# Layer 1's first head: three projections in one group, the gate after them

## The chip, the cores and the metric

The kernel runs on one core of a Trainium2 chip. The metric is the device time of one execution in microseconds (us); a comparison is the ratio of two such times. TensorE multiplies matrices, VectorE, ScalarE and GpSimd work on tiles, SyncE's queue starts the transfers. In the rows of the profile they are PE (PEld is its weight load), DVE, ACT, POOL and SP.

## The reference

Two layers of a hybrid decoder act on 512 prompt tokens and 32 sample tokens (8 sequences of 4), 544 columns in all, with a model width of 1024. Layer 0 is block-sparse attention beside a convolution branch and one output projection. Layer 1, where the change lies, is a gated linear recurrence with eight heads of 128 channels. Cut to what matters here:

```
h = rms(x, norm_1)
q, fz, i, g = split(h @ w_in_1, [1024, 1024, 1024, 1024])
f = lb + (1 - lb) * sigmoid(fz);  kk = 1 - f;  qq = silu(q);  vv = i
o, S = scan(qq, kk, log f, vv, S0)          # chunks of 64 tokens, per head
y = x + (rms(o, o_norm_1) * silu(g)) @ w_out_1
```

For each head the four projections (q at column 0, forget gate f at 1024, value v at 2048, output gate g at 3072) are 1024 by 128 matrices applied to all 544 columns.

## The kernel before

Activations lie transposed, channels on the 128 partitions and tokens along the free axis, in two halves of 272 columns. A projection is done by `unit(w, a, hf)` for one half: 24 matmuls of 128x128 by 272 columns that add up in one PSUM bank of the tag g. There are three per block of 128 input channels: high part of the weights by high part of h, high by low, low by high. Tag g has three banks, used in turn, so a unit waits until the unit three places before it has been read out of its bank.

`wtile` brings one weight matrix in: a transfer into `wr`, the rounded high part `wh` by ScalarE (L133), the rest `wl` by VectorE (L134). Each of the three has three buffers, used in turn, so a `wh` conversion waits until the last matmul that read the matrix three places before it.

The end of layer 0 sets how layer 1 starts. Half 0 of x is finished first and normalized (`normed`, L167 and L105/L106) while the output projection of half 1 runs. Half 1 is not normalized at first: h holds x times the norm's weight, split raw (L645, L646), and the scale per token, `r1b`, comes when the sum of squares has gone through one matmul with ones (L655), a square root on ScalarE (L656) and a reciprocal (L657). So in the first head of layer 1 each result of half 1 is scaled on its way out of PSUM (L745, which writes a tile named `sg`). After the first head `normed(lp, "n1", r1b, 1)` (L749) overwrites half 1 of h with the normalized values, eight blocks of each part, which the second head needs.

`proj(hd)` runs four jobs in two groups of two. In each group it goes by halves: job a half 0, job b half 0, job a half 1, job b half 1:

```
jobs = ((1024, ep_f), (0, ep_q), (2048, ep_v), (3072, ep_g))
for grp in (jobs[:2], jobs[2:]):
```

What follows a unit is its `ep_` function. `ep_f` and `ep_q` need ScalarE's sigmoid (L714, L720), `ep_v` is a plain copy (L735), `ep_g` a sigmoid and a product (L731, L732). The sigmoid is in another table of ScalarE than the square root of L656 and the exponential of L673 (a small softmax for `lb`); a table is loaded by an ACT_TABLE_LOAD.

`scan(hd)` is the recurrence. It starts with products on VectorE (L771 to L810), then come four runs of small matmuls (L818, L824, L826, L829: `kk` by `qy`, `kv` by `qx`, the sample states), then VectorE multiplies `kk` and `qq` by decays for rising block sizes (L888, L887), ScalarE keeps copies of them at two sizes (L851, L852) and scales the eight sample states (L930, after L829), and more small matmuls follow (L859 and on). GpSimd does one product `ve` (L932) per head, after `vx` (L707).

The order on each engine is fixed when the kernel is built: a scheduler follows the program's order as priority and places each instruction where its own timing model finds it ready. Engines run their lists in order. The order printed for a kernel tells what stands behind what; no time is read from it.

Of the kernel before, what the change touches and what calls it, by code (L numbers as in the profile page):

```python
# [66 lines left out]
def hybrid_step(ctx, tc, xt_in, cache_kt, cache_v, conv_in, hgrn_in, page_table, par_in, k_norm_0,  # L67
# [15 lines left out]
    def mk(pool, tag, shape, bufs, dt=F32):  # L83
        return pool.tile(shape, dt, name=nm(tag), tag=tag, bufs=bufs)

    def bank(tag, cols=512, dt=F32):
        return pp.tile([128, cols], dt, name=nm(tag), tag=tag, bufs={"g": 3, "s": 2, "t": 2, "o": 1}[tag])
# [13 lines left out]
    def transpose(out, in_, np_):  # L101
        PE.transpose(out, in_, ident[:np_, :np_])  # L102
# [24 lines left out]
    def wtile(w, col, k0=0, k1=KT):  # L127
        nk = k1 - k0
        raw = mk(wp, "wr", [128, nk, 128], 3)
        SP.dma_start(raw, w[col // 128, :, k0:k1, :])  # L130
        wh = mk(wp, "wh", [128, nk, 128], 3, F32R)
        wl = mk(wp, "wl", [128, nk, 128], 3, F32R)
        A.activation(wh, raw, AF.Copy)  # L133
        V.tensor_tensor(wl, raw, wh, op=ALU.subtract)  # L134
        return wh, wl, k0, k1

    def unit(w, a, hf):
        ps = bank("g", HALF)
        wh, wl, k0, k1 = w
        for k in range(k0, k1):  # L140
            ah, al = a[0][hf][k], a[1][hf][k]
            PE.matmul(ps, wh[:, k - k0, :], ah, start=(k == k0), stop=False)  # L142
            PE.matmul(ps, wh[:, k - k0, :], al, start=False, stop=False)  # L143
            PE.matmul(ps, wl[:, k - k0, :], ah, start=False, stop=(k == k1 - 1))  # L144
        return ps
# [18 lines left out]
    def normed(pool, g, rb, hf):  # L164
        for k in range(KT):
            tmp = mk(pool, "tb", [128, HALF], 3)
            V.scalar_tensor_tensor(tmp, xT[k][:, HC[hf]], vec(g, k), rb, op0=ALU.mult, op1=ALU.mult)  # L167
            split(hh_[k][:, HC[hf]], hh_[KT + k][:, HC[hf]], tmp)
# [5 lines left out]
    def mtile(key, dt=F32R):  # L174
        m_[key] = mk(hp, "m", [128, T], 2 * KT, dt)
        return m_[key]
# [486 lines left out]
    with tc.tile_pool(name="l1", bufs=1) as lp:  # L663
# [34 lines left out]
        def rep4(out, src, los, n, raw=None):  # L698
            r4 = mk(lp, "r4", [128, 4, TS], 2)
            G.tensor_copy(r4, src[:, TP:T].unsqueeze(1).to_broadcast([128, 4, TS]))  # L700
            pv = bank("t", 128)
            transpose(pv, r4.rearrange("p a t -> p (a t)"), 128)
            if raw is not None:
                V.tensor_copy(raw[:TS], pv[:TS])
            A.activation(out, pv, AF.Copy)
            for l in los:
                V.tensor_tensor(out[l:l + n], pv[l:l + n], out[l:l + n], op=ALU.subtract)  # L707

        def proj(hd):
            f, kk, qq = mk(lp, "f", [128, T], 2), mk(lp, "kk", [128, T], 2), mk(lp, "qq", [128, TP], 2)  # L710
            gg, vT = mtile(("gg", hd), F32), mtile(("vT", hd), F32)

            def ep_f(ps, hs):
                A.activation(f[:, hs], ps, AF.Sigmoid)  # L714

            qx = mk(lp, "qx", [128, T // 32, 80], 2)

            def ep_q(ps, hs):
                sg = mk(lp, "sg", [128, HALF], 4)
                A.activation(sg, ps, AF.Sigmoid)  # L720
                o = hs.start
                for a, b in ((0, 256), (256, 272)) if o == 0 else ((0, 16), (16, 272)):
                    n = max(1, (b - a) // 32)
                    t0 = (o + a) % 32
                    i0 = (o + a) // 32
                    V.tensor_tensor(qx[:, i0:i0 + n, t0:t0 + (b - a) // n], sg[:, a:b].rearrange("p (n t) -> p n t", n=n),
                                    ps[:, a:b].rearrange("p (n t) -> p n t", n=n), op=ALU.mult)

            def ep_g(ps, hs):
                sg = mk(lp, "sg", [128, HALF], 4)  # L730
                A.activation(sg, ps, AF.Sigmoid)  # L731
                V.tensor_tensor(gg[:, hs], sg, ps, op=ALU.mult)  # L732

            def ep_v(ps, hs):
                A.activation(vT[:, hs], ps, AF.Copy)  # L735

            jobs = ((1024, ep_f), (0, ep_q), (2048, ep_v), (3072, ep_g))
            for grp in (jobs[:2], jobs[2:]):
                ws = [wtile(w_in_1, col + hd * 128) for col, _ in grp]
                for hf in range(2):  # L740
                    for w, (_, ep) in zip(ws, grp):
                        ps = unit(w, h, hf)
                        if hd == 0 and hf:
                            raw = mk(lp, "sg", [128, HALF], 4)
                            V.tensor_tensor(raw, ps, r1b, op=ALU.mult)  # L745
                            ps = raw
                        ep(ps, HC[hf])
            if hd == 0:
                normed(lp, "n1", r1b, 1)  # L749
            V.tensor_scalar(f, f, lbm[:, 5, hd:hd + 1], lbm[:, 4, hd:hd + 1], op0=ALU.mult, op1=ALU.add)  # L750
            G.tensor_scalar(kk, f, -1.0, 1.0, op0=ALU.mult, op1=ALU.add)
            vt = mk(lp, "vt", [128, 512], 2)
            pv = bank("t")
            for i in range(4):
                transpose(pv[:, i * 128:(i + 1) * 128], vT[:, i * 128:(i + 1) * 128], 128)
            A.activation(vt, pv, AF.Copy)
            vs = VS[hd % 2]
            vx = mk(lp, "vx", [128, 128], 2, F32R)
            rep4(vx, vT, (32, 96), 32, vs)
            return f, kk, qx, qq, vt, vs, vx, gg  # L760
# [211 lines left out]
        for hd in range(KT):  # L972
            args = proj(hd)
            if prev is not None and hd < KT - 1:
                drain(prev)
            cur = scan(hd, *args)
            if hd == KT - 1:
                drain(prev, cur)
            else:
                for _ in range(6 if hd == KT - 2 else 9):  # L980
                    next(cur)
            prev = cur
# [69 lines left out]
```

## Time and profile before

| | us |
|---|---|
| median of 3 runs (lowest, highest) | 666.47 (664.44, 666.55) |
| the profiled execution | 668.9 |
| its span, first to last instruction | 667.1 |
| TensorE busy in the span | 639.3 (96%) |
| VectorE / ScalarE / GpSimd busy | 522.9 / 361.8 / 69.8 |

The mean granted TensorE clock of the profiled execution is 0.987 of full speed. The durations below come from this execution; its time is 2.4 us above the median of the runs.

In the rows a matmul's time is modelled: 0.29 us for one of 272 columns although the next starts 0.125 us later. A unit is therefore read from start to start. An instruction of ScalarE or VectorE likewise overlaps the next one by some 0.1 us.

### The profile page before, as it was taken

Reading aid. Unit: us, or ns where it says so; the run is one execution under the profiler, and the core shown is the slowest. Engines: PE = TensorE matmul, PEld = TensorE weight load, DVE = VectorE, ACT = ScalarE, POOL = GpSimd, SP = SyncE. Lnnn points to the kernel's source line nnn. Section 1 sums busy time; section 2 is a strip of 40 time slices with the busy share of each in tenths; the row PEclk is TensorE's granted clock in tenths of the full one; section 3 lists DMA queues with packets and bytes.
Section 4 is the critical chain, followed back from the end, with each engine's and each line's share of the span. In section 5 each row is a group of like instructions: output and inputs, shape, how many; then the busy total and the mean of one; then the engine's idle time right before and its main releaser. Section 6 shows DMA issues by size and latency. Waiting matters only on the chain.

```text
span 667.1 us, 14861 instructions
## 1 busy us (share of the span) xinstructions
PE 639.3 (96%) x5806; PEld 583.3 (87%) x5806; DVE 522.9 (78%) x1238; ACT 361.8 (54%) x906; POOL 69.8 (10%) x95
## 2 busy tenths in 40 slices
PE   8899999989988899999998999999999999999997
PEld 6799999968867885657998999999999999999997
DVE  6999999899954973444896988787878787866656
ACT  7333444736557879533665654646464646447321
POOL 6000120000101100000001202020202020111000
PEclk9899999979999999989998999999999999999999
DMA  9422343132121160574453123141323232323114
GB/s 260 155 90 64 99 141 111 34 97 65 49 80 32 32 209 1 191 235 173 149 187 133 65 64 132 64 132 64 132 64 132 65 132 64 116 68 100 45 57 146
DMA packets 34584, 70.57 MB, mean 106 GB/s; under 512 B 7378, under 2 KB 16082, under 8 KB 34514
## 3 DMA queue, kind: packets, MB, share of 16 engines
q1 hardware_dynamic: 34514, 69.62, 32.6%
q8 instruction: 46, 0.75, 0.5%
q14 instruction: 24, 0.20, 0.1%
HBM read 59.88 MB, written 9.73 MB: 104 GB/s over the span
## 4 chain that ended last, share of the span: by engine, by line
PE 87%; ACT 4%; DVE 3%; DMA 3%; SPq 1%; issue 1%; POOL 0%; DVEq 0%; POOLq 0%
PE g L142 23%; PE g L143 22%; PE g L144 22%; PE t L102 5%; PE s L470 2%; PE o L493 2%; PE s L622 2%; DMA kn<-in_cache_kt_dram 1%; DMA wr<-in_w_in_dram 1%; PE o L923 1%; PE t L910 1%; PE s L818 1%; DMA xTall<-in_xt_dram 1%; PE s L824 1%; PE o L925 1%; PE s L587 1%
## 5 line engine op out<-in xcount | busy, mean ns | idle before, releaser
L142 PE MATMUL g<-h,wh 128*128 128x272 f32 x944 | 278.6, 296 | 7.3 <-ACT f L714 2.6
L143 PE MATMUL g<-h,wh 128*128 128x272 f32 x944 | 276.4, 293 | 1.8 <-DVE h L273 1.8
L144 PE MATMUL g<-h,wl 128*128 128x272 f32 x944 | 274.2, 291 | 0.0
L142 PEld LDWEIGHTS g<-h,wh 128*128 128x128 f32 x944 | 179.9, 191 | 11.3 <-ACT f L714 3.1
L143 PEld LDWEIGHTS g<-h,wh 128*128 128x128 f32 x944 | 179.6, 190 | 4.4 <-DVE h L273 2.9
L144 PEld LDWEIGHTS g<-h,wl 128*128 128x128 f32 x944 | 179.8, 191 | 0.3 <-issue 0.2
L133 ACT ACTIVATE wh<-wr 128x1024 fp32r<-128x1024 f32 (+4 forms) x90 | 88.1, 981 | 104.9 <-PE g L143 93.2
L134 DVE TENSOR_TENSOR wl<-wr,wh 128x1024 fp32r<-128x1024 f32 (+4 forms) x90 | 100.9, 1122 | 28.4 <-ACT wh L133 27.6
L516 DVE SCALAR_TENSOR_TENSOR m<-m,vecs,m 128x512 f32<-128x512 f32 x120 | 84.0, 734 | 0.1
L144 PE MATMUL g<-m,wl 128*128 128x272 f32 x256 | 73.9, 291 | 0.0
L142 PE MATMUL g<-m,wh 128*128 128x272 f32 x256 | 73.5, 294 | 0.0
L143 PE MATMUL g<-m,wh 128*128 128x272 f32 x240 | 69.6, 291 | 0.0
L142 PEld LDWEIGHTS g<-m,wh 128*128 128x128 f32 x256 | 47.4, 188 | 5.9 <-issue 3.8
L144 PEld LDWEIGHTS g<-m,wl 128*128 128x128 f32 x256 | 48.1, 188 | 0.2
L143 PEld LDWEIGHTS g<-m,wh 128*128 128x128 f32 x240 | 45.1, 188 | 2.9 <-DVE mx L601 1.5
L478 DVE TENSOR_REDUCE mx<-s 128x1 f32<-128x128 f32 (+3 forms) x32 | 15.5, 483 | 15.6 <-PE s L472 15.5
L930 ACT ACTIVATE S<-S,tot 128x128 f32<-128x128 f32 x64 | 20.5, 390 | 11.4 <-PE t L829 11.4
L470 PE MATMUL s<-kz,qT 128*128 128x128 f32 (+3 forms) x64 | 23.5, 451 | 0.2
L887 DVE TENSOR_TENSOR qq<-qq,tot 128x256 f32<-128x256 f32 x24 | 11.5, 479 | 14.9 <-PE s L859 12.0
L488 ACT ACTIVATE PT<-t 128x128 f32<-128x128 f32 (+3 forms) x32 | 13.7, 433 | 14.6 <-PE t L102 14.5
L932 POOL TENSOR_TENSOR ve<-vx,cst 128x1024 fp32r<-128x1024 f32 x8 | 16.3, 2038 | 49.6 <-DVE vx L707 30.0
L991 DVE TENSOR_TENSOR xTall<-g,xTall 128x272 f32<-128x272 f32 x32 | 13.5, 437 | 8.7 <-PE g L144 8.3
(300 smaller groups left out, 1037.3 us busy)
## 6 DMA issues: line engine op xcount, KB each, us to landing
wr<-in_w_in_dram SPq DMA_DIRECT2D x58, 512.0 KB, 3.6
wr<-in_w_out_dram SPq DMA_DIRECT2D x16, 512.0 KB, 3.6
kn<-in_cache_kt_dram SPq DMA_DIRECT2D x16, 256.0 KB, 3.3
kn<-in_cache_v_dram SPq DMA_DIRECT2D x16, 256.0 KB, 4.2
S<-in_hgrn_dram SPq DMA_DIRECT2D x8, 512.0 KB, 4.6
out_hgrns_dram<-S SPq DMA_DIRECT2D x8, 512.0 KB, 2.8
xTall<-in_xt_dram SPq DMA_DIRECT2D x8, 272.0 KB, 5.3
out_y_dram<-xTall SPq DMA_DIRECT2D x8, 272.0 KB, 3.1
```

Of the source, the lines that this page charges most:

```text
L102: PE.transpose(out, in_, ident[:np_, :np_])
L133: A.activation(wh, raw, AF.Copy)
L134: V.tensor_tensor(wl, raw, wh, op=ALU.subtract)
L142: PE.matmul(ps, wh[:, k - k0, :], ah, start=(k == k0), stop=False)
L143: PE.matmul(ps, wh[:, k - k0, :], al, start=False, stop=False)
L144: PE.matmul(ps, wl[:, k - k0, :], ah, start=False, stop=(k == k1 - 1))
L470: PE.matmul(ss[hh][:, :L], qT[:, i * 128:(i + 1) * 128], kT[:, hh, 0:L], start=True, stop=False)
L478: V.tensor_reduce(mx[:, 0:1], s[:, :L], axis=AX.X, op=ALU.max, negate=True)
L488: A.activation(PT[:, :L], pT[:, :L], AF.Copy)
L516: V.scalar_tensor_tensor(cy[c][:, :TP], up[c][:, j:j + TP], cw[:, c, j:j + 1], cy[c][:, :TP], op0=ALU.mult, op1=ALU.add)
L930: A.activation(S0[:, n], S0[:, n], AF.Copy, scale=tots[:, n:n + 1])
L932: G.tensor_tensor(ve, vx.unsqueeze(1).to_broadcast([128, NS, 128]), exm.unsqueeze(2).to_broadcast([128, NS, 128]), op=ALU.mult)
```

## The change

For the first head of layer 1 alone (hd = 0) the two groups become one of three jobs, value, forget gate, query, and one of the gate alone. The other heads keep (f, q) and (v, g).

```diff
             jobs = ((1024, ep_f), (0, ep_q), (2048, ep_v), (3072, ep_g))
-            for grp in (jobs[:2], jobs[2:]):
+            for grp in (jobs[:2], jobs[2:]) if hd else ((jobs[2], jobs[0], jobs[1]), jobs[3:]):
                 ws = [wtile(w_in_1, col + hd * 128) for col, _ in grp]
                 for hf in range(2):
                     for w, (_, ep) in zip(ws, grp):
```

Units of the first head in order, before: f0 q0 f1 q1 v0 g0 v1 g1 (the digit is the half). Now: v0 f0 q0 v1 f1 q1 g0 g1. With three banks, q1 waited for f0's bank before; now v1 follows v0, f1 follows f0 and q1 follows q0. No instruction of the arithmetic is added or removed. The order of all engines changes from here on.

In the names below, h_80 to h_87 are the high parts of h's eight blocks and h_88 to h_95 the low parts; a number after a name is a tile's own number.

ScalarE at the turn from layer 0 to layer 1. Before; wh_4401 is the weight of g, f_4261 the result of f0, sg_4330 that of q0:

```order
L133 ACTIVATE wh_4401<-wr_4399 128x1024
L656 ACTIVATE r1b<-t_4218,eps 128x272
L714 ACT_TABLE_LOAD
L714 ACTIVATE f_4261<-g_4279 128x272
L720 ACTIVATE sg_4330<-g_4305 128x272
L673 ACT_TABLE_LOAD
L673 ACTIVATE lbm<-lbm 128x16
```

Now, where wh_4455 is the weight of g and wh_4778 the second head's weight of f:

```order
L656 ACTIVATE r1b<-t_4218,eps 128x272
L714 ACT_TABLE_LOAD
L714 ACTIVATE f_4261<-g_4311 128x272
L720 ACTIVATE sg_4362<-g_4337 128x272
L673 ACT_TABLE_LOAD
L673 ACTIVATE lbm<-lbm 128x16
L133 ACTIVATE wh_4455<-wr_4453 128x1024
```

The conversion of g's weight moved from ahead of the square root to behind the exponential; the table load and f0's sigmoid stay behind the square root.

VectorE during the second head's first units, where half 1 of h is normalized for it. Before (each h here is a low part, L106):

```order
L106 TENSOR_TENSOR h_92<-tb_4533,h_84 128x272
L834 COPY_PREDICATED AD_4241<-lvt,s_4595 128x128
L837 COPY_PREDICATED AS_4243<-lvt,s_4595 32x32
L106 TENSOR_TENSOR h_93<-tb_4537,h_85 128x272
L888 TENSOR_TENSOR kk_4262<-kk_4262,tot_4651 128x32x8
L167 SCALAR_TENSOR_TENSOR tb_4541<-xTall,vecs,r1b 128x272
L167 SCALAR_TENSOR_TENSOR tb_4545<-xTall,vecs,r1b 128x272
```

Now:

```order
L106 TENSOR_TENSOR h_92<-tb_4533,h_84 128x272
L707 TENSOR_TENSOR vx_4558<-t_4561,vx_4558 32x128 x2
L775 TENSOR_TENSOR qy_4570<-qx_4266,f_4261 128x17x8
L890 TENSOR_TENSOR tot_4654<-tot_4651 128x32
L106 TENSOR_TENSOR h_93<-tb_4537,h_85 128x272
L167 SCALAR_TENSOR_TENSOR tb_4541<-xTall,vecs,r1b 128x272
L726 TENSOR_TENSOR qx_4775<-sg_4839,g_4814 128x8x32
```

The pair L707, after which GpSimd's product `ve` starts, moved from behind h_93 to between h_92 and h_93. On TensorE the first matmul with h_93 now stands eight rows behind the first with h_92.

ScalarE in the second head's projections, where the scan of the first head has its part. Before; wh_4906 is the second head's weight of g, f_4770 its forget gate (g_4843 is the bank of its f1):

```order
L930 ACTIVATE S_4577<-S_4577,tot_4586 128x128 x2
L705 ACTIVATE vx_4558<-t_4561 128x128
L714 ACTIVATE f_4770<-g_4788 128x272
L851 ACTIVATE kv_4656<-kk_4262 128x256
L852 ACTIVATE kv_4663<-qq_4263 128x256
L105 ACTIVATE h_86<-tb_4541 128x272
L105 ACTIVATE h_87<-tb_4545 128x272
L720 ACTIVATE sg_4839<-g_4814 128x272
L851 ACTIVATE kv_4663<-kk_4262 128x256
L133 ACTIVATE wh_4906<-wr_4904 128x1024
L714 ACTIVATE f_4770<-g_4843 128x272
```

Now:

```order
L105 ACTIVATE h_86<-tb_4541 128x272
L105 ACTIVATE h_87<-tb_4545 128x272
L852 ACTIVATE kv_4656<-qq_4263 128x256
L851 ACTIVATE kv_4656<-kk_4262 128x256
L852 ACTIVATE kv_4663<-qq_4263 128x256
L930 ACTIVATE S_4577<-S_4577,tot_4586 128x128 x6
L831 ACTIVATE c_4579<-t_4596 128x128
L930 ACTIVATE S_4577<-S_4577,tot_4586 128x128 x2
L133 ACTIVATE wh_4906<-wr_4904 128x1024
L714 ACTIVATE f_4770<-g_4843 128x272
```

The eight scalings of the first head's sample states stood well ahead of the conversion of wh_4906; now they stand directly ahead of it.

TensorE at the same place. Before, the second head's g0 (bank g_4936) begins here, 45 rows after the last matmul of f1 (bank g_4843):

```order
L142 MATMUL g_4910<-h_87,wh_4900 128x272
L143 MATMUL g_4910<-h_95,wh_4900 128x272
L144 MATMUL g_4910<-h_87,wl_4901 128x272
L923 MATMUL o_4742<-vt_4551,AT_4242 128x128 x2
L142 MATMUL g_4936<-h_80,wh_4906 128x272
```

Now the scan's small matmuls stand ahead of the last three matmuls of f1; after the rows shown come nine matmuls of v0 (g_4910), and then the first of g0, `L142 MATMUL g_4936<-h_80,wh_4906 128x272`:

```order
L818 MATMUL s_4594<-qy_4570,kk_4262 32x56 x16
L824 MATMUL s_4595<-qx_4266,kv_4580 32x80 x16
L826 MATMUL s_4595<-qx_4266,kv_4580 32x80
L829 MATMUL t_4596<-S_4577,QS_4245 32x128 x8
L142 MATMUL g_4843<-h_87,wh_4778 128x272
L143 MATMUL g_4843<-h_95,wh_4778 128x272
L144 MATMUL g_4843<-h_87,wl_4779 128x272
L143 MATMUL g_4869<-h_94,wh_4784 128x272
L144 MATMUL g_4869<-h_86,wl_4785 128x272
L142 MATMUL g_4869<-h_87,wh_4784 128x272
L143 MATMUL g_4869<-h_95,wh_4784 128x272
L144 MATMUL g_4869<-h_87,wl_4785 128x272
```

The scan's first matmuls moved back by some 90 rows, behind most of the second head's f1 and q1, and g0 moved to within 17 rows of them.

## Rows read from the trace of the kernel before

**Rows 1.** Busy by stretch: length, PE, PEld, DVE, ACT, POOL, PEclk, DMA share, GB/s.

```profile
211.00:216.00 5.00, 2.65 (x12) 1.48 (x11) 4.42 (x10) 3.35 (x8) 2.60 (x3) 1.00 0.00 0
285.10:288.50 3.40, 3.40 (x61) 1.69 (x53) 1.14 (x4) 0.59 (x2) 0.00 (x0) 0.51 0.39 128
353.20:355.80 2.60, 0.03 (x1) 0.00 (x0) 2.44 (x5) 2.57 (x5) 2.15 (x12) 1.00 0.57 128
356.80:360.20 3.40, 3.40 (x17) 3.40 (x16) 2.17 (x8) 0.82 (x2) 0.00 (x0) 0.50 0.74 301
361.68:376.46 14.78, 14.78 (x190) 14.57 (x188) 13.96 (x41) 8.96 (x19) 3.97 (x4) 1.00 0.21 72
363.60:660.00 296.40, 296.40 (x3233) 283.72 (x3233) 232.86 (x683) 155.61 (x480) 40.30 (x46) 1.00 0.27 89
```

**Rows 2.** TensorE's waits by releaser (us in total, times, longest): layer 1, then two of layer 0.

```profile
PE g L142 <- ACT f L714: 2.6, 1, 2.6
...
PE t L540 <- POOL kn L538: 4.1, 2, 2.2
...
PE s L587 <- DMA kn<-in_cache_kt_dram: 1.5, 1, 1.5
```

**Rows 3.** Timeline, ScalarE at the turn: start, us, instruction, idle before and releaser.

```profile
352.68 1.06 ACT L133 ACTIVATE wh<-wr 128x1024 fp32r<-128x1024 f32 x1 [3.08 <-PE g L143]
353.64 0.47 ACT L656 ACTIVATE r1b<-t,eps 128x272 f32<-128x272 f32 x1
354.13 1.28 ACT L714 ACT_TABLE_LOAD   x1
355.42 0.40 ACT L714 ACTIVATE f<-g 128x272 f32<-128x272 f32 x1
```

**Rows 4.** Timeline, TensorE: first unit of layer 1, L655, and after the wait.

```profile
343.62 0.29 PE L142 MATMUL g<-h,wh 128*128 128x272 f32 x1
...
352.61 0.62 PE L655 MATMUL t<-tb,ones 128*128 128x272 f32 x2
...
355.87 0.39 PE L142 MATMUL g<-h,wh 128*128 128x272 f32 x1 [2.65 <-ACT f L714]
...
356.88 0.43 PE L143 MATMUL g<-h,wh 128*128 128x272 f32 x1
...
360.06 0.37 PE L142 MATMUL g<-h,wh 128*128 128x272 f32 x1
```

**Rows 5.** Chain of work that ended last: start, us, what (L655's use for half 0 first).

```profile
324.77 0.46 PE t L655 x2
...
372.70 0.22 PE t L102 x2
...
375.01 0.53 PE s L818 x32
...
376.15 0.51 PE t L829 x12
```

**Rows 6.** Timeline, VectorE: a weight's low part, `kk`, and a product that was held.

```profile
361.68 1.23 DVE L134 TENSOR_TENSOR wl<-wr,wh 128x1024 fp32r<-128x1024 f32 x1 [0.53 <-ACT wh L133]
...
377.76 0.41 DVE L888 TENSOR_TENSOR kk<-kk,tot 128x256 f32<-128x256 f32 x1
...
408.72 1.86 DVE L114 SCALAR_TENSOR_TENSOR sd<-sd 128x5 f32<-128x5 f32 x1
```

**Rows 7.** Timeline, GpSimd in the last of these stretches.

```profile
408.49 2.06 POOL L932 TENSOR_TENSOR ve<-vx,cst 128x1024 fp32r<-128x1024 f32 x1 [4.96 <-DVE vx L707]
```

**Rows 8.** Timeline, ScalarE in a later head: copy, state scalings, the next weight.

```profile
414.19 0.40 ACT L852 ACTIVATE kv<-qq 128x256 f32<-128x256 f32 x1
...
416.77 1.87 ACT L930 ACTIVATE S<-S,tot 128x128 f32<-128x128 f32 x6 [1.84 <-PE t L829]
...
419.29 1.04 ACT L133 ACTIVATE wh<-wr 128x1024 fp32r<-128x1024 f32 x1
```

**Rows 9.** The page, part 6: weight transfers, count, KB each, median us to landing.

```profile
wr<-in_w_in_dram SPq DMA_DIRECT2D x58, 512.0 KB, 3.6
```

## The prediction

> **What bounds the kernel now.** I read the stretches first, then TensorE's waits, then the timelines of the engines at the wait. From 363.6 to 660 us TensorE is busy in every one of 296.40 us at full clock, while VectorE works 232.86 and ScalarE 155.61 of them [rows 1]. So layer 1 is bound by TensorE, and only two things can change its time there: a stretch in which TensorE stands, and one in which its clock is low. Before the change layer 1 has one of each. The wait is that of q1 for the bank of f0, 2.6 us [rows 2]. It is not the arithmetic that is late: f0's sigmoid stands on ScalarE behind the conversion of g's weight, which itself waits for f1's end, behind the square root of L656 and behind a table load [rows 3]. The clock follows: from 356.80 to 360.20 the granted clock is 0.50, that is 1.2 instead of 2.4 GHz, after TensorE had stood for those 2.65 us [rows 1, 4].
>
> **The change, part by part.** The sum is made on the profiled execution, 668.9 us.
>
> *The wait at q1.* A unit's matmuls follow each other every 0.125 us: 72 of them lie between 343.62 and 352.61 [rows 4]. The bank that is needed third is now that of v0, whose plain copy needs no table and can run at once. So v1 starts without a wait and the old 2.65 us are gone. But f1, one unit later, needs f0's bank, and f0's sigmoid still stands behind the square root. Let L655 start at S. It ends 0.62 later [rows 4]; from the start of the square root to the restart of TensorE it took 355.87 - 353.64 = 2.23 [rows 3, 4]. So f1 can start at S + 2.85. TensorE meanwhile has L655 itself (0.46), the last eight matmuls of v1 (1.0) and two transposes (0.22) [rows 5], 1.68 in all. A wait of **1.2** stays where there were 2.65: **-1.45**. L655 itself is not late: with 88 rows ahead of it instead of 72 it falls 2.0 us later, and the squares that it sums are done before.
>
> Around this table load the trace shows no more than the load: it starts 0.02 us after the square root ends, takes 1.28, and the sigmoid starts 0.01 us behind it [rows 3].
>
> The Trainium skill (ScalarE: Activation LUTs, "What ACT_TABLE_LOAD costs") puts a switch of tables at about 1283 ns for the load and 1380 ns more for a drain, 2.66 us together. The trace agrees on the load and shows no drain. By that page the wait at f1 would be 2.6 and the sum 1.4 us higher.
>
> *The clock behind it.* Between 356.88 and 360.06 fourteen matmuls start every 0.227 us [rows 4]. In 3.4 us at that pace 15 are done, each 0.102 late: 1.5 us. TensorE stood 2.2 us at L540 in layer 0, and the stretch around it shows full clock; it stood 1.5 us at L587, and 0.51 followed [rows 1, 2]. So a short wait may or may not lower it; 1.2 us is less than either, and I count the clock as kept: **-1.5**.
>
> *The vector queue of the second head.* f, q and with them the first head's scan are later by a unit or two, so VectorE has the scan's products, the raw results' scaling and the normalization of h together. From the conversion of g's weight (behind the exponential on ScalarE, about 360.3) to h_92 I count 42 instructions; with the durations of the same instructions in this trace, less about 0.08 us overlap each, they take 16.7 us. The stretch 361.68 to 376.46 holds 41 instructions in 13.96 us, one weight conversion less [rows 1]; so 15.2 to 16.7. TensorE reaches h_92 at about 378.7 by unit lengths: a lead of 1.6, up to 3. Then GpSimd's product of 2.06 us starts after L707, and a vector instruction that meets it is held until it ends: a tiny one took 1.86 [rows 6, 7]. So h_93 comes 1.4 + 1.8 us after h_92, and TensorE wants it eight matmuls, 1.0 us, after h_92. Bounds: 0 (lead of 2.2 or more) and 2.2 (no lead). My count says 0.5 there and 0.3 more for the bank of q0, read on the same engine (L726): **+0.8**.
>
> *The second head's gate.* This is the dear one. Its g0 needs the rounded and the rest part of its weight. The conversion on ScalarE waits for f1's last matmul and stands directly behind the first head's eight state scalings, and those behind two copies that wait for VectorE, which waits for L818. From the start of L818: L818 0.53 [rows 5]; two products on `kk`, 0.41 each less overlap, 0.74 [rows 6]; two copies, L851 and L852 of 0.40 less overlap, 0.65; the scalings up to the conversion's start, 419.29 - 416.77 = 2.52; the conversion 1.04 [rows 8]; the rest part 1.23 [rows 6]; and six handoffs of about 0.05 (f0's sigmoid ends at 355.82, TensorE starts at 355.87 [rows 3, 4]). Together 6.95. On TensorE L818 to L829 take 1.65 [rows 5], then 17 matmuls (2.1) and two of g0 that need the rounded part alone (0.25): 4.0. So TensorE stands for **+2.9** in all, whenever L818 starts. Nothing else can fill it: v1 needs a bank that is read out later still. Before, 65 rows lay between the end of the same small matmuls and f1's last rows, and the scalings were done long before.
>
> *The clock there.* A gap of 2.9 us, only two matmuls in it, is longer than the 2.65 after which 0.50 was granted [rows 1, 4]: **+1.5** if it falls again, 0 if not. I take the fall, since the nearest row is that one.
>
> *What costs nothing.* SyncE's queue holds the transfers of the scan's constants and states behind L655, so they go out 2 us later, with the second head's v and g weights behind them; these wait for the wr buffers anyway. The weight of v goes out when g's weight is split, lands 3.6 us later [rows 9], and is needed some 4 us after that. GpSimd's list only changes order; its one effect is the product above. From the third head on the order is the old pattern, shifted, with no instruction more.
>
> Sum: -1.45 - 1.5 + 0.8 + 2.9 + 1.5 = +2.25, 671.15 for the profiled execution. The median of the runs lies 2.4 lower; I add the same difference to it: 666.47 + 2.25 = **668.7**, +0.34%.
>
> **The rivals.** (All on the median.)
>
> 1. *The gate unit waits, the clock stays.* 668.7 - 1.5 = 667.2. For it: full clock around the wait of 2.2 in layer 0. Against: 2.65 was enough in this very stage.
> 2. *The gate unit hardly waits,* because the chain from L818 to the weight is shorter than I reckon; it must shrink from 6.95 to 4.0 to vanish. 666.47 - 1.45 - 1.5 + 0.8 = 664.3, on the fast side. For it: in the trace of before the scalings never held TensorE. Against: there they stood far ahead, and every piece of the chain has a row.
> 3. *Both waits lower the clock,* or the vector queue is held for its full 2.2: 668.7 + 1.5 = 670.2, with both 671.6.
> 4. *The change does just what it says:* no wait at f1, none later. 666.47 - 2.65 - 1.5 = 662.3. Against: f0's sigmoid still stands behind the same square root.
> 5. *The table load also waits for the pipe to run dry.* As a mechanism here: a wait at f1 longer by as much as another load, 1.28 [rows 3], 670.0. The two rows around the load speak against it. The skill's page named above would have it so.
>
> **How the numbers follow.** Chances: forecast 0.50 (668.7; with its bounds 667.9 to 670.1), rival 1 0.17, rival 2 0.13, rival 3 0.13, rival 4 0.05, rival 5 0.02. A measurement of this kernel tells about 0.3%, 2.0 us, from no change. Slower by more, above 668.5: about 0.31 of the forecast's 0.50, all of 3 and 5, a little of 1: 0.48. Faster by more, below 664.5: rival 4 and 0.08 of rival 2: 0.13. Between: 0.39. The range, 664.4 to 671.2, leaves out rival 4, the lower half of 2 and the upper end of 3, about 0.15. Cases of both signs hold chances, so the forecast's own range stands beside it: 667.9 to 670.1.
>
> **What would show it.** In the profile after: no wait at q1; one of about 1.2 us at f1 put down to ScalarE L714; the granted clock at full after it; a wait or two under 1 us on VectorE L106 or L726 some 23 us later; then, at the first matmuls of the second head's gate, about 2.9 us put down to ScalarE L714 or L133 and VectorE L134, with the scalings L930 just ahead on ScalarE, and 3.4 us at half clock. From there to the end TensorE without a gap. What would make it wrong: a gap in the steady heads, which the order alone doesn't show; ScalarE reaching the conversion before the scalings are through; or a clock that doesn't follow the gap.

## The result and the profile after

The kernel after takes **673.23 us** (median of 6 runs, 669.63 to 674.15), the kernel before beside it 665.46 (6 runs, 663.02 to 667.93): 1.0095 times as long, 95% interval 1.0068 to 1.0122. A second series of 12 runs gave 671.92 beside 667.17, and 1.0060 (1.0037 to 1.0083). So it is slower, as forecast, but by 4 to 6 us by these ratios where 2.25 were forecast, and both medians lie above the range (664.4 to 671.2).

The profiled execution of after is its 673.52 us run. Busy by stretch, as in [rows 1] (length, PE, PEld, DVE, ACT, POOL, PEclk, DMA share, GB/s): where the old wait was, the new one, the second head's gate with its half clock, and the rest.

```profile
353.20:355.80 2.60, 2.60 (x22) 2.52 (x20) 0.82 (x4) 0.91 (x2) 0.86 (x5) 1.00 0.00 0
356.00:360.00 4.00, 2.94 (x24) 2.88 (x24) 2.04 (x5) 3.79 (x6) 1.10 (x7) 1.00 0.80 286
...
390.10:393.50 3.40, 3.00 (x13) 3.01 (x14) 3.40 (x7) 1.18 (x3) 0.75 (x1) 0.51 0.51 154
...
393.60:660.00 266.40, 263.82 (x2906) 251.74 (x2906) 194.84 (x600) 139.95 (x436) 33.34 (x40) 1.00 0.27 88
```

TensorE now stands 1.06 us behind 356.00 (4.00 less 2.94) and the clock stays up there. It falls to 0.51 at 390.10. And the last row has what [rows 1] did not: in the steady heads TensorE is idle for 2.58 us. Its waits in layer 1 after (us in total, times, longest), against the single one of 2.6 in [rows 2]:

```profile
PE g L142 <- ACT f L714: 3.1, 2, 2.1
PE t L910 <- ACT ktk L904: 2.5, 4, 0.8
PE g L144 <- DVE wl L134: 0.5, 1, 0.5
PE g L142 <- DVE qx L726: 0.3, 1, 0.3
PE g L143 <- DVE h L106: 0.2, 1, 0.2
```

The first row holds the 1.06 at the first head's f1 and 2.06 at the second head's gate. How the latter comes about is in ScalarE's timeline (start, us, instruction, idle before), with TensorE's two restarts below it:

```profile
385.33 0.40 ACT L852 ACTIVATE kv<-qq 128x256 f32<-128x256 f32 x1
385.64 1.85 ACT L930 ACTIVATE S<-S,tot 128x128 f32<-128x128 f32 x6
387.40 0.25 ACT L831 ACTIVATE c<-t 128x128 f32<-128x128 f32 x1
387.56 0.68 ACT L930 ACTIVATE S<-S,tot 128x128 f32<-128x128 f32 x2
388.14 1.04 ACT L133 ACTIVATE wh<-wr 128x1024 fp32r<-128x1024 f32 x1
389.09 0.38 ACT L714 ACTIVATE f<-g 128x272 f32<-128x272 f32 x1
...
389.51 0.39 PE L142 MATMUL g<-h,wh 128*128 128x272 f32 x1 [2.06 <-ACT f L714]
...
390.50 0.59 PE L144 MATMUL g<-h,wl 128*128 128x272 f32 x1 [0.47 <-DVE wl L134]
```

The eight state scalings stand ahead of the gate's weight (1.04) and of f1's sigmoid, whose bank TensorE needs; then the weight's low part is late too. That is 2.53 us.

The new kind of wait, L910 for `ktk`, is one of the steady heads. First the kernel after, for the third head's scan, ScalarE and then TensorE:

```profile
464.66 0.92 ACT L873 ACTIVATE AD<-s 16x64 f32<-16x64 f32 x4
465.60 1.46 ACT L878 ACTIVATE AT<-s 32x64 f32<-32x64 f32 x6
466.96 0.96 ACT L898 ACTIVATE AT<-AD 32x128 f32<-32x128 f32 x3
...
469.11 1.04 ACT L133 ACTIVATE wh<-wr 128x1024 fp32r<-128x1024 f32 x1
470.06 0.38 ACT L735 ACTIVATE m<-g 128x272 f32<-128x272 f32 x1
470.33 0.59 ACT L904 ACTIVATE ktk<-t 128x512 f32<-128x512 f32 x1
...
470.98 1.16 PE L910 MATMUL t<-vt,ktk 128*128 128x128 f32 x8 [0.57 <-ACT ktk L904]
```

In the kernel before (second head; the later ones repeat it) the copy ends 1.0 us ahead of its use, at 426.89 and 427.91:

```profile
426.31 0.58 ACT L904 ACTIVATE ktk<-t 128x512 f32<-128x512 f32 x1
...
427.91 1.05 PE L910 MATMUL t<-vt,ktk 128*128 128x128 f32 x8
```

The program order says much of why. Between the transposes that `ktk` copies and L910 stand 35 matmuls of projection units in the kernel before, in every steady head, and in the kernel after 10 in the second head and 13 from the third on. The count alone does not decide it: the second head after, with 10, has no wait.

```profile
437.17 0.60 ACT L904 ACTIVATE ktk<-t 128x512 f32<-128x512 f32 x1
...
437.82 1.16 PE L910 MATMUL t<-vt,ktk 128*128 128x128 f32 x8
```

There the next weight's conversion (L133) comes on ScalarE behind the copy, at 437.96; in the third head one of 1.04 stands ahead of it, at 469.11. So few rows leave no room, and what stands ahead of the copy on its own engine uses it up.

The scans run later against the projections. In the steady heads L818 keeps its place, but L859 comes behind 159 of a head's 192 projection matmuls in place of 85, and the transposes behind 179 in place of 102. I put this down to the first head, without a test of each part: its f and q come behind v's units now, VectorE has the normalization of h beside the scan's products, and the first L818 starts at 383.42, 13.95 us behind the second head's first unit (369.47), and before at 374.94, 2.26 behind it (372.68).

### The profile page after: what moved, and what is told of

Same layout as the page of the kernel before. It is cut to its first block, busy times and chain, and to the rows that moved or that the text cites. A ratio compares the mean times of both kernels' runs of the same rounds, so it can differ in the third digit from the quotient of the medians.

```text
span 671.6 us, 14880 instructions
## 1 busy us (share of the span) xinstructions
PE 639.2 (95%) x5806; PEld 583.2 (87%) x5806; DVE 514.4 (77%) x1238; ACT 363.7 (54%) x906; POOL 71.2 (11%) x95
## 4 chain that ended last, share of the span: by engine, by line
PE 80%; DVE 9%; ACT 5%; DMA 3%; issue 1%; SPq 1%; POOL 0%; DVEq 0%; ACTq 0%
PE g L142 21%; PE g L144 20%; PE g L143 20%; PE t L102 4%; PE s L470 2%; DMA kn<-in_cache_kt_dram 2%; DVE m L516 2%; PE o L493 1%; PE s L622 1%; PE t L910 1%; DVE wl L134 1%; ACT wh L133 1%; PE o L923 1%; DMA wr<-in_w_in_dram 1%; PE s L824 1%
## 5 line engine op out<-in xcount | busy, mean ns | idle before, releaser
L142 PE MATMUL g<-h,wh 128*128 128x272 f32 x944 | 278.6, 296 | 8.1 <-ACT f L714 3.1
L142 PEld LDWEIGHTS g<-h,wh 128*128 128x128 f32 x944 | 180.0, 191 | 12.4 <-ACT f L714 3.6
L133 ACT ACTIVATE wh<-wr 128x1024 fp32r<-128x1024 f32 (+4 forms) x90 | 88.0, 980 | 108.6 <-PE g L143 97.9
L142 PE MATMUL g<-m,wh 128*128 128x272 f32 x256 | 73.8, 295 | 0.0
L142 PEld LDWEIGHTS g<-m,wh 128*128 128x128 f32 x256 | 47.4, 188 | 5.8 <-issue 3.6
L887 DVE TENSOR_TENSOR qq<-qq,tot 128x256 f32<-128x256 f32 x24 | 10.0, 419 | 23.7 <-ACT kv L852 21.2
```

## The experiments

Layer 0 and the end of the program differ from execution to execution: the cache pages' wait (L587) is 1.0 us in e4 and 2.4 in after, and the clock falls in other places. So beside the timed ratio I give a **stretch** from each profile: from the start of layer 1's first matmul to the end of TensorE's last one. For the kernel before it is 662.53 - 343.62. The ratio is to runs of the kernel before in the same series; their median moves between 665.46 and 667.17, so medians of different rows are less sure than ratios.

| kernel | stretch, us | waits in it | half clock in it | median, us | ratio (95%) |
|---|---|---|---|---|---|
| before, first profile | 318.91 | 2.65 | yes | 665.46 | 1 |
| e1 before again | 317.42 | 2.65 | no | 666.01 | 0.9995 (0.9975 to 1.0014) |
| after, first profile | 323.51 | 6.6 | yes | 673.23 | 1.0095 (1.0068 to 1.0122) |
| e5 after again | 323.72 | 6.4 | yes | 671.92 | 1.0060 (1.0037 to 1.0083) |
| e2 after, scalings late | 319.27 | 4.1 | no | 668.54 | 1.0037 (1.0020 to 1.0054) |
| e4 after, ktk on VectorE | 322.66 | 4.0 | yes | 670.60 | 1.0062 (1.0040 to 1.0084) |
| e8 after, both waits out | 318.95 | 3.8 | no | 667.20 | 1.0003 (0.9976 to 1.0029) |
| e3 before, pairs v f, q g | 320.04 | 4.8 | no | 667.88 | 1.0036 (1.0018 to 1.0054) |
| e6 before, scan late | 320.93 | 6.4 | no | 670.83 | 1.0047 (1.0021 to 1.0074) |
| e7 before, root late | 316.87 | 2.3 | no | 664.87 | 0.9956 (0.9935 to 0.9978) |
| e10 the same again | 318.15 | 2.3 | yes | 664.60 | 0.9986 (0.9964 to 1.0008) |
| e9 root and conversion late | 315.87 | 0.8 | no | 664.87 | 0.9982 (0.9965 to 1.0000) |
| e11 the same again | 316.01 | 0.9 | no | 663.59 | 0.9954 (0.9930 to 0.9977) |

### The two kernels again (e1, e5)

> The kernel before, unchanged, profiled and timed once more. Theory A (the carry from one profiled execution was a term of the sum: the execution that the prediction was built on had four falls of the granted clock, and a usual one has fewer): the time of this profile is 663 to 668 us, the falls that it shows are not the same four as before, and each fall fewer goes with about 1.5 us less; the fall behind the wait at the second queries unit (clock 0.5 in 356.8 to 360.2 of the first profile) is there again, since the 2.6 us wait ahead of it is. Theory B (the first profile is usual and the median of the prediction's page was luck): four falls in the same places, 668 to 669 us, and a median of the timed runs near 668. Ratio to the kernel before 1.000 by both, within 0.3%.

> The kernel after, unchanged, profiled and timed once more beside the others. Theory (the gap to the kernel before is made of waits and of one clock fall that come in every execution, while the waits for the cache pages in layer 0 and the other falls come and go): the second head's wait of 2.06 us and the recurring waits of L910 (2.5 us in 4) are there again to 0.2 us, the fall behind the second head's wait too, and the median is 669.5 to 673.5, a ratio of 1.006 to 1.010. Rival (the six runs of the changed kernel were slow by luck, as the profile of the kernel before was): 667 to 669, a ratio of 1.001 to 1.004.

Before: the same wait, but behind it the clock did not fall. Its one row of waits, and the 3.4 us behind it:

```profile
352.90:356.30 3.40, 3.40 (x27) 3.40 (x28) 2.84 (x8) 1.96 (x4) 0.00 (x0) 1.00 0.96 375
```

27 matmuls at full clock, 17 in the same stretch of [rows 1]. Without that fall, and with fewer in layer 0, this execution took 663.52. So I was wrong that the fall belongs to that wait. Of the five profiles here with a wait of 2.3 to 2.65 us at this place (before, e1, e6, e7, e10) two show it. After: the waits came again, and half clock from 389.0 on; it follows the second head's two waits in all three profiles that have them (after, e4, e5).

### The second head's wait (e2)

```
-                for _ in range(6 if hd == KT - 2 else 9):
+                for _ in range(6 if hd == KT - 2 else 9 if hd else 8):
...
-                A.activation(f[:, hs], ps, AF.Sigmoid)
+                gate[0] = A.activation(f[:, hs], ps, AF.Sigmoid)
...
+                with (ExitStack() if hd else behind(gate[0])):
+                    A.activation(S0[:, n], S0[:, n], AF.Copy, scale=tots[:, n:n + 1])
```

> The kernel after, with one change: the eight scalings of the first head's state (L930) are held on ScalarE behind the second head's second forget-gate sigmoid, so that the weight conversion and that sigmoid come ahead of them. Theory A (the second head's wait of 2.06 us is these scalings standing ahead of the conversion, 8 x 0.3 us, and the clock falls because of it): the wait at the second head's unit is under 0.5 us, the granted clock does not fall at 390, and the time is 2.0 to 4.0 us under the changed kernel's 673.2, so 669 to 671, a ratio of 1.005 to 1.009 to the kernel before by the earlier 665.5. The recurring wait of L910 for the copy ktk should shrink too, since TensorE's order has 15 matmuls in place of 10 between the transposes and L910: 0 to 1 us in place of 2.5. Rival B (the three-weight group itself costs, through its buffers, and the sigmoid would wait for the conversion anyway): the wait only moves to the weight (wl L134), still over 1.5 us, the clock falls as before, time 672 to 674.

TensorE's waits in layer 1 (same columns):

```profile
PE t L910 <- ACT ktk L904: 2.3, 4, 0.8
PE g L142 <- ACT f L714: 1.1, 1, 1.1
```

The 2.06 are gone, the 0.5 for the low part stayed, the clock stayed up, and the stretch is 4.24 us shorter than after's, the median 3.4 to 4.7. The scalings ahead of the conversion were the cause. (The edge needs the step of the scan that holds them to come behind the second head's projections in the program, which is the first line of the edit; the other instructions of that step move with them.) That L910 would wait less was wrong: 15 matmuls stand there in the second head, but 9 to 13 from the third on.

### The copy on VectorE (e4)

```
-            A.activation(ktk, pk, AF.Copy)
+            (V.tensor_copy(ktk, pk) if 0 < hd < KT - 2 else A.activation(ktk, pk, AF.Copy))
```

> The kernel after, with the copy ktk (L904) of the heads 2 to 6 on VectorE in place of ScalarE; TensorE's order stays the same. Theory A (the recurring wait of L910, 2.5 us in 4, is the copy standing behind some 16 copies of ScalarE, and only 10 matmuls come between the transposes and L910): the wait of L910 falls under 1 us and the time falls by 1.5 to 2.5 us against the changed kernel's 673.2, to 670.7 to 671.7. Rival B (the wait is the transposes' own distance, so that any engine is late; VectorE has a weight's low part of 1.2 us ahead of the copy): L910 waits as long for VectorE, 2 to 4 us in all, and the time stays at 673 or rises by up to 1.5 us.

No wait of L910 is left, and yet the time is not measurably lower (1.0062 against e5's 1.0060; the interval overlaps that of the first series too), the stretch by 0.85 us. One period of a steady head shows it (columns of [rows 1]); before, after, and this kernel:

```profile
437.57:470.79 33.22, 33.22 (x374) 31.55 (x374) 26.82 (x80) 18.58 (x59) 4.84 (x6) 1.00 0.30 97
...
503.54:537.16 33.62, 33.05 (x374) 31.52 (x373) 25.38 (x79) 18.47 (x59) 4.69 (x6) 1.00 0.29 97
...
500.76:534.27 33.51, 33.50 (x375) 31.72 (x374) 25.97 (x81) 18.34 (x58) 4.68 (x6) 1.00 0.31 98
```

Where the wait is gone TensorE is busy for 0.45 us more with the same matmuls, but not in the same order, as I had expected. At the turn to the next head, after and then e4:

```profile
503.54 0.49 PE L818 MATMUL s<-qy,kk 128*32 128x56 f32 x20
504.60 1.16 PE L910 MATMUL t<-vt,ktk 128*128 128x128 f32 x8 [0.56 <-ACT ktk L904]
505.51 0.48 PE L936 MATMUL t<-ve,kts 128*128 128x512 f32 x1
505.92 0.39 PE L818 MATMUL s<-qy,kk 128*32 128x56 f32 x12
...
500.76 0.39 PE L818 MATMUL s<-qy,kk 128*32 128x56 f32 x12
501.16 1.16 PE L910 MATMUL t<-vt,ktk 128*128 128x128 f32 x8
502.25 0.40 PE L818 MATMUL s<-qy,kk 128*32 128x56 f32 x14
502.63 0.49 PE L936 MATMUL t<-ve,kts 128*128 128x512 f32 x1
503.05 0.30 PE L818 MATMUL s<-qy,kk 128*32 128x56 f32 x6
```

Up to the next projection matmul (506.24 and 503.28) these 41 matmuls take 2.70 us after, 0.56 of it the wait, and 2.52 in e4 without one. In e4 fourteen of L818 stand between L910 and L936. From start to start the steps from L910 to L818 and from L818 to L936 take 0.20 us each; after's one step from L910 to L936 takes 0.03. So of the 0.56 that the copy gave back the new order took 0.38, and this run does not show what the wait alone is worth. The price of the late scan is the longer period, 33.5 to 33.6 in place of 33.2 to 33.3 (33.9 where the wait is 0.85), which is less than the wait that is listed in it.

### The late scan without the group of three (e6, e3)

e6 leaves before's groups as they are and only holds the first products of the first head's scan:

```
-                V.tensor_tensor(gg[:, hs], sg, ps, op=ALU.mult)
+                late[0] = V.tensor_tensor(gg[:, hs], sg, ps, op=ALU.mult)
...
+                with (ExitStack() if hd else tc.issue_after(late[0].ins)):
+                    V.tensor_tensor(lag(qx, l), lag(qx, l - 1)[:, :, :, 1:], f4[:, :, :, 1:5 - l], op=ALU.mult)
```

> The kernel before, its groups as they were, with one edge more: the first head's scan starts on VectorE only behind the product of the first head's gate (the last unit of that head), so that the scan of every head runs about as late against the projections as it does in the kernel after. Theory A (what recurs in the kernel after is this lag of the scan, not the group of three as such): L910 waits for ktk again, 1.5 to 2.8 us in about 4 waits, the stretch from the last head's first unit to the output projection's second pass is 1.5 to 2.5 us longer than in the kernel before, the wait of 2.6 us at the second queries unit stays, and the time is 2.5 to 5 us over the kernel before: ratio 1.004 to 1.008. Rival B (the lag costs nothing, and the group of three does it): no waits of L910 over 0.2 us, ratio 0.998 to 1.002.

```profile
PE t L911 <- ACT ktk L905: 3.3, 5, 0.9
PE g L142 <- ACT f L714: 2.7, 1, 2.7
```

The wait for `ktk` (L905 here) appears without any change of groups, with 13 matmuls between the transposes and L911 from the second head on, and the ratio of 1.0047 is in theory A's range. So what recurs in the kernel after is the lag of the scan. Its price in the whole stretch is 3.51 us over e1 (320.93 less 317.42), of which 0.45 is a wait for AD at L928 that the kernel after does not have. From the sixth head's first unit to the eighth's first the kernel before takes 66.50 us, this one 67.58, after 67.52. The end grows too, as expected: from the last head's first unit to TensorE's last matmul it takes 90.45 us before and 92.96 in e6 and in after. A part of these 2.5 us is scan work that the lag only moves there.

e3 has the values first, but two pairs:

```
-            for grp in (jobs[:2], jobs[2:]):
+            for grp in (jobs[:2], jobs[2:]) if hd else ((jobs[2], jobs[0]), (jobs[1], jobs[3])):
```

> The kernel before with the first head's four projections in other pairs: values and forget gate as the first pair, queries and gate as the second (no group of three). Theory A (what gains in the change is that the values' units, whose evacuation needs no sigmoid, fill the time of the square root and the table loads; what loses is the order that the group of three brings to the second head, with the scalings L930 ahead of its conversion): the wait near 356 is under 1 us, no wait of over 1 us near 387, the recurring wait L910 for ktk 0 to 1.5 us (TensorE has 14 matmuls between transposes and L910), and the time is 0 to 3 us under the kernel before: ratio 0.995 to 1.001. Rival B (values first costs by itself, because the gates come later and the scan starts later, so that the phase of the scan against the projections is what loses): ratio 1.006 to 1.010 as with the group of three, with the same recurring wait of about 0.6 us per head.

Neither ratio came: the second head does not wait, but the scan is late here too, L910 waits 2.4 us in 4, and the ratio is 1.0036. One wait for f0's sigmoid (L714) is left in the first head, 1.06 us as in after.

### Both named waits out (e8)

The edit of e2, and the square root moved:

```
             PE.matmul(pr_, ones, sacc, start=True, stop=True)
-            A.activation(r1s[hf], pr_, AF.Sqrt, scale=1.0 / D, bias=eps)
-            V.reciprocal(r1s[hf], r1s[hf])
             if hf == 0:
+                A.activation(r1s[hf], pr_, AF.Sqrt, scale=1.0 / D, bias=eps)
+                V.reciprocal(r1s[hf], r1s[hf])
...
+                    if hd == 0 and hf and grp[0][0] == 2048:
+                        A.activation(r1b, pr_, AF.Sqrt, scale=1.0 / D, bias=eps)
+                        V.reciprocal(r1b, r1b)
```

> The kernel after with both named waits taken away: the square root and reciprocal of the second half moved behind the first half's sigmoids (as in the run of the kernel before with that edit), and the first head's scalings L930 held behind the second head's second forget-gate sigmoid. Theory A (the late scan costs by itself, with its waits of L910 and at the last head): 0.5 to 1.2 us under the run with L930 alone, so 667.3 to 668.1, still over the kernel before by 0.1 to 0.3%, and over the kernel before with the late square root by 3 us or more. Rival B (the two waits are the whole of the loss): 663 to 664.5, level with the kernel before with the late square root.

```profile
PE t L913 <- ACT ktk L907: 2.1, 4, 0.6
PE g L143 <- DVE h L106: 1.3, 1, 1.3
```

Nearer to theory A: 667.20 is 0.1 us under its range and 2.7 above B's. That it is slower than before the runs do not show (1.0003), only the stretch does (318.95 against e1's 317.42), and it lies 2.3 us over e7 where 3 or more were expected. The wait at f1 is gone, but most of it came back on VectorE, as 1.27 us for the normalized h (L106), and the late scan's waits are all there.

### The wait at q1 without moving the values (e7, e9, e10, e11)

e7 and e10 make the edit of the square root on the kernel before (for the group with column 1024).

> The kernel before, its groups as they were, with only the second half's square root and reciprocal moved behind the first half's two sigmoids (in program order into the first head's projections), which costs one table load more on ScalarE. Theory A (the wait of 2.6 us at the second queries unit is the first forget-gate sigmoid standing behind the square root and its table load, and it can be taken away without moving the values, so that the scan keeps its place): no wait over 0.3 us at 345 to 360, no waits of L910, and 2.0 to 3.2 us less: ratio 0.995 to 0.997. Rival B (the wait only moves: the second half's units wait for the square root behind a second table load): a wait of 1 to 2.5 us at the values' or the gate's first unit, ratio 0.998 to 1.001.

> The kernel before with only the late square root, once more, on the same chip as the run with the conversion held too. Its first profile showed 0.4 us less between the start of the first layer's output projection and the last matmul than a profile of the kernel before without a fall there, while the timed runs showed 0.44% (2.3 us between the medians). Theory A (the wait is still there, 2.3 in place of 2.65 us, and the rest was a chance of how many clock falls the runs had): ratio 0.997 to 1.000. Rival B (the shorter wait keeps the clock up, a fall of 1.5 us that the kernel before has in part of its runs): ratio 0.994 to 0.997, and no fall of the granted clock at 350 to 362.

The wait stayed at 2.27 in both. So e7's ratio of 0.9956 is theory A's, but not by its reason; e10's is 0.9986, and its half clock from 352.4 on speaks against rival B. ScalarE's timeline in e7:

```profile
351.41 1.06 ACT L133 ACTIVATE wh<-wr 128x1024 fp32r<-128x1024 f32 x1 [3.09 <-PE g L143]
352.49 1.28 ACT L714 ACT_TABLE_LOAD   x1
353.78 0.40 ACT L714 ACTIVATE f<-g 128x272 f32<-128x272 f32 x1
354.08 0.39 ACT L720 ACTIVATE sg<-g 128x272 f32<-128x272 f32 x1
354.49 1.28 ACT L742 ACT_TABLE_LOAD   x1
```

The square root is out of the way, but the gate weight's conversion still stands ahead of the sigmoid and waits 3.09 us for TensorE. e9 and e11 hold it behind the first queries sigmoid as well:

```
+        with (tc.issue_after(after.ins) if after is not None else ExitStack()):
             A.activation(wh, raw, AF.Copy)
...
+                ws = [wtile(w_in_1, col + hd * 128, after=first[0] if hd == 0 and col == 3072 else None) for col, _ in grp]
```

> The kernel before, its groups as they were, with the late square root (as in the run with that edit alone) and one edge more: the conversion of the first head's gate weight on ScalarE is held behind the first queries sigmoid. In the run with the late square root alone the wait of 2.3 us stayed, because that conversion stood ahead of the sigmoids on ScalarE and waited until TensorE had done with the forget gate's weight (at 351.41), with a table load of 1.28 us behind it. Theory A (two things stood ahead of the first sigmoid, the square root and the conversion, and both have to go): no wait over 0.3 us at 340 to 362, no waits of L910 over 0.2 us, 2.0 to 3.0 us under the run with the late square root alone, so 662 to 663 and a ratio of 0.991 to 0.994. Rival B (the second half's units then wait for the square root, which now stands behind the sigmoids, a table load and the reciprocal of 1.85 us): a wait of 1 to 2.5 us at the gate's first unit, ratio 0.995 to 0.998.

> The kernel before with the late square root and the held conversion, once more, to settle whether it beats the kernel before. Its first profile lay 1.9 us under a profile of the kernel before without a clock fall there, from the start of the first layer's output projection to the last matmul, and its runs 0.18% under it (interval 0.9965 to 1.0000). Theory A (the shorter wait, 0.5 in place of 2.65 us, is a gain in every execution): ratio 0.996 to 0.999, the interval under 1. Rival B (it is hidden by what differs from execution to execution, the falls and the pages' waits in layer 0): ratio 0.999 to 1.001.

e9's waits in layer 1, and the sigmoid:

```profile
PE g L143 <- ACT f L715: 0.5, 1, 0.5
PE t L102 <- POOL r L701: 0.3, 1, 0.3
...
348.12 1.28 ACT L715 ACT_TABLE_LOAD   x1
351.77 0.40 ACT L715 ACTIVATE f<-g 128x272 f32<-128x272 f32 x1 [2.37 <-PE t L656]
...
351.77 0.17 DVE L671 TENSOR_TENSOR lbm<-vecs 128x8 f32<-128x8 f32 x1 [3.04 <-PE t L656]
```

The scan keeps its place, the wait is 0.49, and the stretch is 1.4 to 1.55 us under e1's. The timed runs gave far less than I expected in the first series (0.9982, interval up to 1.0000, a median equal to e7's) and 0.9954 with the interval under 1 in the second, more than expected. This version beats the kernel after, and the one before by 0.2 to 0.5%, clear of the noise in one series of two.

## Why the prediction was right and wrong

- **The wait at q1 turns into one at f1 of 1.2**: 1.06. Right; the bank's release and the start of the square root were the right rows.
- **No drain beside the table load**: right. In e7 too the load starts 0.02 us behind the sigmoid's end and the sigmoid 0.01 behind the load's. The Trainium skill's further 1380 ns (ScalarE: Activation LUTs, "What ACT_TABLE_LOAD costs") appear in no run here. Where ScalarE is idle behind a load, as for 2.37 us in e9, the profile names a matmul as the releaser.
- **The clock behind it, -1.5**: not wrong for that execution, wrong as a term for the median. The fall behind the wait at q1 comes in some executions (two profiles of five), so a usual run had less to give back.
- **The vector queue, +0.8**: 0.15 and 0.27, 0.42. The product that holds it is there: from 377.41 a 128x32 product takes 1.89 us beside GpSimd's 2.05.

```profile
377.41 1.89 DVE L890 TENSOR_TENSOR tot<-tot 128x32 f32<-128x32 f32 x1
...
377.21 2.05 POOL L932 TENSOR_TENSOR ve<-vx,cst 128x1024 fp32r<-128x1024 f32 x1 [0.62 <-DVE vx L707]
```

  The Trainium skill (SBUF — State Buffer, "Who interferes with whom") says that a vector instruction with both inputs in SBUF contends with GpSimd reading there; the row agrees.
- **The second head's gate, +2.9**: 2.06 + 0.47 = 2.53, and e2 shows its cause to be the one named. **The clock there, +1.5**: it fell; 13 matmuls in that stretch, 0.102 us late each, are 1.3.
- **"From the third head on the order is the old pattern, shifted, with no instruction more"**: this step failed. The count of instructions is the same, but the scan is late against the projections, and with it the copy that L910 needs. From the second head's first L818 to the seventh's it is 167.73 us (403.33 to 571.06) where it was 166.28 (404.29 to 570.57): 1.45 us, costed at nothing; over the whole stretch e6 puts the lag at some 3 us. I compared what stands in the lists and not how far a producer stands ahead of its consumer; 35 rows against 13 could be read before the run, though not yet the wait. The prediction did name a gap in the steady heads as a sign of being wrong, but gave it no price and no chance, and the measured medians lie above every case that it priced (671.6 at most). That layer 1's time can change only by a wait or a low clock was too narrow as well: in e4 the order of the same matmuls changed it.
- **The carry to the median** failed too. I took 2.4 us off, since the profiled execution of before lay that far above its median; it had a fall that not every run has, and after's profile lies at its own median. With before at e1's stretch the terms make -1.59 + 0.42 + 2.53 + 1.33 + 1.45 = 4.14 us of after's 6.09. With e6's price for the lag, 3.51 less the 0.45 that after does not have, in place of 1.45 they make 5.75. That rests on single profiles; the other 0.34 us are not placed.

## What to carry to other kernels

Where a change delays one stage of a software pipeline, count for each copy how many rows lie between its producer and its consumer in the later stages, and what stands ahead of the copy on its own engine: a lag set once recurs in every turn. A wait of the bound engine can have several things in front of its releaser; move those (here the root and the conversion) before moving the work. And set a sum on a stretch that holds no term that comes and goes, such as a clock fall seen in one execution.

## What the runs showed of the hardware

A wait taken away is not yet time won where the order changes with it: in e4 the same 41 matmuls, in a different order, lost 0.38 us of the 0.56, at hand-overs between small matmuls of different shapes that took 0.20 us each in place of one of 0.03. At the place of the old wait, 2.65 us of waiting were followed by half clock in one profile of three (before, not e1 and e6) and 2.27 us in one of two (e10, not e7). And in e9 the sigmoid, its table loaded at 349.40 and its unit's last row some 48 rows earlier on TensorE, started only with the end of the sum's matmul at 351.77. The trace names that matmul as its releaser, and VectorE's L671, which needs neither, starts at the same moment. Both write into tiles of layer 1's pool, which the program opens when it has closed layer 0's, where the operand of that matmul lies. That they wait for this memory fits both rows, but no run tests it.
